# One-hot matrices of an expert-weight spread: token by token with contiguous columns, in place of four tokens interleaved

## The chip, the cores and the metric

The kernel runs on one core of one Trainium2 chip. A core has a matrix engine (TensorE; PE in the profile, with its weight loads listed apart as PEld), a vector engine (VectorE, DVE), a scalar engine (ScalarE, ACT), GpSimd (POOL) and a queue engine that issues most transfers (SyncE, SP). Each engine works through its own list of instructions in the order in which they stand and waits on semaphores. The metric is the device time of one execution in microseconds, lower being better; the time of a kernel is the median of three runs.

## The reference

Two transformer blocks run over 512 tokens of 1024 channels, in float32. The change lies in the last part of the second block, a product-key expert layer. For each token eight heads each choose 16 of 128 x 128 = 16384 experts, and each choice has a softmax weight:

```python
    s = jnp.einsum('thpd,pkd->thpk', q, sub_keys).astype(jnp.float32)
    s_top, i_top = lax.top_k(s, K)
    cand = (s_top[:, :, 0, :, None] + s_top[:, :, 1, None, :]).reshape(T, PEER_HEADS, K * K)
    cand_idx = (i_top[:, :, 0, :, None] * PEER_N_KEYS + i_top[:, :, 1, None, :]).reshape(T, PEER_HEADS, K * K)
    best, pos = lax.top_k(cand, K)
    eidx = jnp.take_along_axis(cand_idx, pos, axis=-1)
    g = jax.nn.softmax(best, axis=-1)
...
        u = expert_u[ib]
        a = jax.nn.gelu(jnp.einsum('thkd,td->thk', u, xb).astype(jnp.float32), approximate=False)
        w = (gb * a).astype(expert_v.dtype)
        return jnp.einsum('thk,thkd->td', w, expert_v[ib])
```

So a token has 128 triples (i, j, g): the two key numbers of an expert and its weight.

## The kernel before

Everything before the expert layer (two feed-forward blocks and two attention mixers) is left as it is. In the expert layer the first 128 tokens (tile 0) fetch their experts' rows one by one (`gather`, lines 1440 to 1458, issued by POOL, each row of products summed on DVE as `junk`). The other three tiles of 128 tokens are done densely: all 16384 experts are multiplied with the 384 tokens, in 128 chunks of 128 experts, and each result is multiplied with the token's weight for that expert, which is zero for most. One chunk is `emit_a`: 1024 weight columns are split into a high and a low part (`whi` on ACT at L120, `wlo` on DVE at L121), then 24 products of 384 columns run on PE (L126 to L128), then comes a gelu on ACT (`ga`).

For the dense part the weights g must lie in memory as a table [expert, token]. `peer_level2` (DVE alone) finds the 128 triples of each token of a tile, and `peer_spread` writes them out. For each token it makes two one-hot matrices with one row per triple: `oi` marks the triple's i, `oj` its j, and `og` is `oj` times g, in two float16 parts. Their product on PE, `oi` transposed times `og`, summed over the two parts, has each g at its place (i, j). DVE makes the matrices for eight tokens at a time by four instructions (`oi`, `oj`, `og` twice). Then PE runs 16 pairs of a weight load (`oi` of a token) and a matmul (`og` of that token, 128 columns) at L1383, ACT copies each four tokens out of PSUM into `gb` (L1386), and SP sends every 16 tokens to memory. That is 768 pairs of load and matmul over three tiles. `oi` and both `og` have two buffers each, `oj` one.

Work is written so that chunks of `emit_a` stand between: six before each tile's `peer_level2`, two after each 16 tokens. A scheduler then sets the order of every engine's list when the program is built; at run time the lists are fixed. The raw weights have two buffers of two chunks each, `whi` and `wlo` three each. After the spread comes the dense loop over 128 chunks, which reads the table back.

Before the change the matrices of four tokens are interleaved: element (token t, column j) of a group of four lies at 4 j + t, so that DVE reads the four tokens' values as a run, and PE reads a token's 128 columns in steps of four elements.

Of the kernel before, what the change touches and what calls it, by code (L numbers as in the profile page):

```python
# [9 lines left out]
F32 = mybir.dt.float32  # L10
F32R = mybir.dt.float32r
BF = mybir.dt.bfloat16
F16 = mybir.dt.float16
# [7 lines left out]
P = 128  # L21
# [60 lines left out]
class Body:  # L82
# [4 lines left out]
    # ---------------------------------------------------------------- helpers  # L87
# [3 lines left out]
    def banks(self, **tags):  # L91
        """Cut the eight PSUM banks into rings."""
        assert sum(tags.values()) == 8
        if self.bank_stack is not None:
            self.bank_stack.close()
        self.bank_stack = ExitStack()
        self.rings = {t: self.pool(self.bank_stack, "psum_" + t, bufs=n, space=PSUM, reuse_waits="tile")
                      for t, n in tags.items()}
# [42 lines left out]
    def rstd(self, ms, width=1, eps=EPS):  # L141
        """(ms + eps)^-1/2 of mean squares."""
# [8 lines left out]
    def sumsq(self, ap, n):  # L151
        """Sum over the row of its squares over n."""
# [5 lines left out]
    def xrstd(self, t):  # L158
        """1 / rms of the rows of x; the column that follows them brings EPS in."""
        return self.rstd(self.sumsq(self.xe[:, t, :D + 1], D), eps=0.0)  # L160

    def diag(self, r):
        """diag(r), as the right side of a transposing product."""
# [7 lines left out]
    # ---------------------------------------------------------------- set-up  # L171
# [88 lines left out]
    # ---------------------------------------------------------------- modulation  # L260
    def mod_unit(self, which, u, fast=False, tag="mod"):
        """256 columns of the modulation product, as columns over partitions."""
# [52 lines left out]
    def acol(self, i, sc, g, ks=slice(0, 8)):  # L315
        """(1 + sc) * g as columns."""
# [3 lines left out]
    def row_out(self, colv, tag="ps"):  # L320
        """A [128, 8] column vector, as a row in DRAM."""
# [9 lines left out]
    def row_in(self, d, tag="grow"):  # L331
        """The row over all partitions."""
# [12 lines left out]
    def begin(self, hi, lo):  # L345
        """Shift and scale of the first norm, h and the first products of the first swiglu,
        256 channels at a time."""
# [54 lines left out]
    # ---------------------------------------------------------------- norms  # L402
# [5 lines left out]
    def transposed(self, src, n, t, hi, lo, scale=None, bias=None, k0=0, tag="ps", diag=None):  # L408
        """src [128 t, n*128] -> hi/lo [128, k, 512 t] at tile t, each k scaled (and shifted) by a column,
        each row scaled by a diagonal matrix where one is given."""  # L410
# [29 lines left out]
    def boundary(self, join, scale, bias, last):  # L440
        """From one product to the next phase: last(t) emits the end of the product of a token tile, join(t)
        its way into x; then x is normed and turned, the second half of it later, by the steps returned."""
# [15 lines left out]
    def postnorm(self, t, y, grow):  # L458
        """x[t] += rms_norm(y) * grow, y two banks."""
# [11 lines left out]
    # ---------------------------------------------------------------- swiglu  # L471
    def ffn(self, gu, dn, h, between, join, scale, bias, ps0=None):
        """join(t, y) takes the two PSUM banks of a token tile; returns the next h and its pending steps."""
        nc = self.nc
        (hi, lo), late_h = h
        with ExitStack() as st:
            pool = self.pool(st, "ffn", reuse_waits="tile")
            # the modulation's weights pass through where the last four chunks will lie
# [64 lines left out]
    # ---------------------------------------------------------------- products  # L543
    def nform(self, ap, x, width, then, kd=KD, late=None):
        """[t, width] = x^T-tiles @ unit; then(t, psum) per token tile. The unit is [p, kd, width].
        The first of a phase goes token tile by token tile, as they come, with the steps that bring them."""
# [20 lines left out]
    def rope(self, src, out, half, j, heads):  # L567
        """src [128, heads, 2*half] (PSUM or SBUF) -> out, tables of tile j."""
# [14 lines left out]
    def attend(self, work, seg, scale, po, mneg, sums, n):  # L583
        """One softmax over one segment (lhsT, rhs, masks, values) as three stages to emit: the
        scores and their exponentials, their transposes, and the product with the values, left unnormalised in po."""
# [33 lines left out]
    def pipeline(self, chains, skews=(0, 3, 4)):  # L619
        """Emit the stages of the chains, each so many chains later; yields in between."""  # L620
# [6 lines left out]
    def merge(self, main, filler, n):  # L627
        """Emit n steps of the filler after each step of main, and what is left of it at the end."""
# [14 lines left out]
    # ---------------------------------------------------------------- first mixer  # L643
    def mixer1(self, u, late):
        """Returns the two branches' outputs [t, .] and the stack that holds them."""
# [47 lines left out]
    def latents(self, ap, cols, u, pa, at, late=None):  # L693
        """Columns of u @ w_in into pa[:, t, at:at+cols]."""
# [4 lines left out]
    def dsa_prep(self, pool, u, qT, kT, vv, qix, kix, wi, late):  # L699
# [4 lines left out]
        # columns: 256 of c_kv | 384 of c_q | k_rope, k_idx, w_idx, zeros  # L704
# [36 lines left out]
    def indexer(self, pool, qix, kix, wi, mk):  # L741
        """Additive masks of the selected keys, of the query blocks past the first."""
# [35 lines left out]
    def k_nope(self, w, kd, x, kT):  # L778
        """Rows 0..63 of every head, two heads at a time."""
# [8 lines left out]
    def q_rope(self, ap, kd, x, qT, qix, pos0):  # L788
        """Rotary parts of all heads (and of the indexer, where qix is given)."""
# [29 lines left out]
    def dilated(self, work, dil, u, ob, more):  # L819
        """Three dilated groups, two heads at a time; yields in between."""  # L820
# [72 lines left out]
    def dil_join(self, work, po, neg, sums, out):  # L893
        """The groups weighed by their shares of the joint softmax."""
# [51 lines left out]
    def gate(self, r, u, p):  # L946
        """One gate of 128 channels; yields in between."""
# [7 lines left out]
    def combine1(self, u, oa, ob, st):  # L955
        """z^T as a pair, then y banks."""
# [48 lines left out]
    def project(self, ap, z, pool, join, scale, bias):  # L1005
        """y = z^T tile @ four units of 256 columns, two banks a token tile; join, scale, bias as in ffn."""
# [26 lines left out]
    # ---------------------------------------------------------------- second mixer  # L1033
    def mixer2(self, h, st, late):
# [4 lines left out]
        # values and gates of the retention are made beside the attention  # L1039
# [665 lines left out]
```

## Time and profile before

| | us |
|---|---|
| median of three runs | 2908.83 |
| the three runs | 2907.96 to 2914.29 |
| span of the profiled execution, first to last instruction | 2905.4 |
| PE busy in it | 2848.4 (98%) |
| DVE busy in it | 2055.1 (71%) |
| ACT busy in it | 1156.0 (40%) |
| POOL busy in it | 368.6 (13%) |

The profile gives the execution's own time as its span alone; the median of the runs lies 3.4 us above it (start and end of the program). Busy time of an engine is the union of its instructions. [...]

### The profile page before, as it was taken

To read this page: it belongs to the slowest core of one execution; us is meant where nothing else is said; L and a number is where in the kernel's file an instruction comes from. 1 tells how busy PE (TensorE), PEld (TensorE's weight loads), DVE (VectorE), ACT (ScalarE), POOL (GpSimd) and SP (SyncE) were. 2 spreads that over 40 slices of the span, in tenths; PEclk is the share of its full clock that TensorE was granted. 3 is DMA by queue.
4 is the path that set the end of the run, shared out by engine and by line. 5 is a ranking of instruction groups with operands and counts; after the bars stand their busy time and mean duration, and the time that the engine had idled before them with its cause. 6 is when DMAs were issued, how large, how long until landed. Compare 5 with 4: busy or idle time off the path is not lost. (4 is left out here: it accounts for less than half of the span.)

```text
span 2905.4 us, 41181 instructions
## 1 busy us (share of the span) xinstructions
PE 2848.4 (98%) x15725; PEld 2454.6 (84%) x15725; DVE 2055.1 (71%) x4416; ACT 1156.0 (40%) x1946; POOL 368.6 (13%) x367
## 2 busy tenths in 40 slices
PE   8999999999999999999999999999999999999998
PEld 6877788878779877888899888999998888989986
DVE  6795246886566786236665799898867778878787
ACT  4343144333534443235422433655543333333333
POOL 0000000000000000001011002111111115444341
PEclk9999999999999999999998999999999999999999
DMA  6663222222042564221122227777889989888885
GB/s 274 226 228 137 92 73 80 73 68 89 16 148 110 207 229 168 99 87 62 55 74 75 93 100 262 267 250 264 283 312 350 324 316 342 337 297 322 310 322 192
DMA packets 152533, 553.09 MB, mean 190 GB/s; under 512 B 12368, under 2 KB 61840, under 8 KB 112400
## 3 DMA queue, kind: packets, MB, share of 16 engines
q1 hardware_dynamic: 111040, 404.25, 38.1%
q0 software_dynamic: 38848, 140.56, 13.6%
q10 hardware_dynamic: 2448, 5.65, 0.5%
q8 instruction: 123, 2.02, 0.3%
q14 instruction: 74, 0.61, 0.1%
HBM read 505.95 MB, written 44.47 MB: 189 GB/s over the span
## 5 line engine op out<-in xcount | busy, mean ns | idle before, releaser
L120 ACT ACTIVATE whi<-raw 128x1024 fp32r<-128x1024 f32 (+2 forms) x491 | 510.2, 1040 | 833.6 <-PE ps L127 405.2
L121 DVE TENSOR_TENSOR wlo<-raw,whi 128x1024 fp32r<-128x1024 f32 (+2 forms) x491 | 588.8, 1200 | 327.0 <-ACT whi L120 318.0
L126 PE MATMUL ps<-h_hi,whi 128*128 128x384 f32 (+2 forms) x1904 | 692.1, 364 | 4.1 <-ACT ga L1431 2.5
L128 PE MATMUL ps<-h_hi,wlo 128*128 128x384 f32 (+2 forms) x1904 | 683.1, 359 | 2.6 <-DVE wlo L121 2.6
L127 PE MATMUL ps<-h_lo,whi 128*128 128x384 f32 (+2 forms) x1904 | 684.3, 359 | 0.8 <-DVE h_lo L132 0.8
L126 PEld LDWEIGHTS ps<-h_hi,whi 128*128 128x128 f32 x1904 | 360.0, 189 | 37.4 <-ACT ga L1431 3.5
L128 PEld LDWEIGHTS ps<-h_hi,wlo 128*128 128x128 f32 x1904 | 359.4, 189 | 34.8 <-DVE wlo L121 3.3
L127 PEld LDWEIGHTS ps<-h_lo,whi 128*128 128x128 f32 x1904 | 360.0, 189 | 31.3 <-DVE h_lo L132 1.0
L128 PE MATMUL acc<-whi,wl 128*128 128x512 f32 x768 | 302.7, 394 | 0.0
L126 PE MATMUL acc<-whi,wh 128*128 128x512 f32 x768 | 302.6, 394 | 0.0
L127 PE MATMUL acc<-wlo,wh 128*128 128x512 f32 x768 | 302.5, 394 | 0.0
L1446 POOL DMA_INDIRECT erow<-in_eu,ids x128 | 142.1, 1110 | 686.0 <-DVE junk L1450 501.0
L131 ACT ACTIVATE wh<-wv 128x384 fp32r<-128x384 f32 x128 | 67.3, 526 | 337.0 <-issue 184.0
L1446 POOL DMA_INDIRECT erow<-in_ev,ids x128 | 167.0, 1305 | 225.1 <-DVE eacc L1458 199.9
L126 PE MATMUL ps<-whi,h_hi 128*128 128x256 f32 (+1 forms) x608 | 186.3, 307 | 0.0
L127 PE MATMUL ps<-wlo,h_hi 128*128 128x256 f32 (+1 forms) x608 | 184.4, 303 | 0.0
L128 PE MATMUL ps<-whi,h_lo 128*128 128x256 f32 (+1 forms) x608 | 184.0, 303 | 0.0
L128 PEld LDWEIGHTS acc<-whi,wl 128*128 128x128 f32 x768 | 143.7, 187 | 35.4
L127 PEld LDWEIGHTS acc<-wlo,wh 128*128 128x128 f32 x768 | 143.7, 187 | 33.4 <-DVE wlo L121 0.2
L126 PEld LDWEIGHTS acc<-whi,wh 128*128 128x128 f32 x768 | 143.6, 187 | 33.3 <-ACT whi L120 0.4
L1458 DVE SCALAR_TENSOR_TENSOR eacc<-erow,wgt,eacc 128x1024 f32<-128x1024 f32 x127 | 162.7, 1281 | 6.0 <-DMA erow<-in_ev,ids 4.4
L290 DVE SCALAR_TENSOR_TENSOR rows<-mraw,sil,rows 128x256 f32<-128x256 f32 x336 | 159.8, 481 | 6.5
(453 smaller groups left out, 4721.4 us busy)
## 6 DMA issues: line engine op xcount, KB each, us to landing
raw<-in_euT SPq DMA_DIRECT2D x64, 1024.0 KB
raw<-in_evp SPq DMA_DIRECT2D x64, 1024.0 KB
raw<-in_gu SPq DMA_DIRECT2D x44, 1024.0 KB
mraw<-in_wmod SPq DMA_DIRECT2D x24, 1024.0 KB
mraw<-in_wada SPq DMA_DIRECT2D x24, 1024.0 KB
dg<-gb SPq DMA_DIRECT2D x24, 1024.0 KB
gt<-dg SPq DMA_DIRECT2D x16, 1536.0 KB
raw<-in_dn SPq DMA_DIRECT2D x22, 1024.0 KB
```

The lines of the kernel that those rows point to most:

```text
L120: self.nc.scalar.activation(hi, r, AF.Copy)
L121: self.last_low = self.nc.vector.tensor_tensor(lo, r, hi.bitcast(F32), op=OP.subtract)
L126: mm(out, l[0], r[0], start=start, stop=False)
L127: mm(out, l[0], r[1], start=False, stop=False)
L128: self.last_mm = mm(out, l[1], r[0], start=False, stop=stop)
L131: self.nc.scalar.activation(hi, v, AF.Copy)
L290: nc.vector.scalar_tensor_tensor(rows, rv[:, k, :], c, rows, op0=OP.mult, op1=OP.add)
L1446: nc.gpsimd.indirect_dma_start(out=row, out_offset=None, in_=src, in_offset=bass.IndirectOffsetOnAxis(ap=ids[:, m:m + 1], axis=0))
L1458: nc.vector.scalar_tensor_tensor(eacc, row, wg[:, m:m + 1], eacc, op0=OP.mult, op1=OP.add)
```

## The change

The matrices of a token now lie in one piece: `oi`, `oj` and `og` are [token, 128 columns] for eight tokens, and PE reads 128 neighbouring columns. For DVE to still read runs of four, the values of a token (`it`, `jt`, `g1`, `g2`) are written four times next to each other when they come out of PSUM, so that these four small instructions are four times as wide (512 in place of 128 elements per partition), and the column numbers `io` are no longer repeated (128 in place of 512). The counts of all instructions stay. The diff's other lines remove comments.

```diff
-        g1 = sp.tile([P, P], F16, name="g1")
-        g2 = sp.tile([P, P], F16, name="g2")
-        nc.scalar.activation(g1, p[:, 256:384], AF.Copy, scale=16384.0)
-        nc.vector.scalar_tensor_tensor(g2, p[:, 256:384], 16384.0, g1, op0=OP.mult, op1=OP.subtract)
-        it, jt = sp.tile([P, P], F16, name="it"), sp.tile([P, P], F16, name="jt")
-        nc.scalar.activation(it, p[:, 0:P], AF.Copy)
-        nc.scalar.activation(jt, p[:, P:2 * P], AF.Copy)
-        ios = io[:, None].to_broadcast([P, 2, P, 4])
+
+        it, jt, g1, g2 = (sp.tile([P, P, 4], F16, name=n) for n in ("it", "jt", "g1", "g2"))
+        four = lambda k: p[:, k * P:(k + 1) * P, None].to_broadcast([P, P, 4])
+        nc.scalar.activation(g1, four(2), AF.Copy, scale=16384.0)
+        nc.vector.scalar_tensor_tensor(g2, four(2), 16384.0, g1, op0=OP.mult, op1=OP.subtract)
+        nc.scalar.activation(it, four(0), AF.Copy)
+        nc.scalar.activation(jt, four(1), AF.Copy)
+        ios = io.rearrange("p (o k f) -> p o k f", o=1, f=4).to_broadcast([P, 8, 32, 4])
...
-                row = [z[:, t0:t0 + 8].rearrange("p (h o t) -> p h o t", h=2, o=1).to_broadcast([P, 2, P, 4])
-                       for z in (it, jt, g1, g2)]
-                new = lambda n, m: sp.tile([P, 2, P, 4], F16, name=n, tag=n, bufs=m)
+                row = [z[:, t0:t0 + 8, None, :].to_broadcast([P, 8, 32, 4]) for z in (it, jt, g1, g2)]
+                new = lambda n, m: sp.tile([P, 8, P], F16, name=n, tag=n, bufs=m)
+                wide = lambda z: z.rearrange("p t (k f) -> p t k f", f=4)
                 oi, oj, og = new("oi", 2), new("oj", 1), [new("og0", 2), new("og1", 2)]
-                nc.vector.tensor_tensor(oi, ios, row[0], op=OP.is_equal)
-                nc.vector.tensor_tensor(oj, ios, row[1], op=OP.is_equal)
-                nc.vector.tensor_tensor(og[0], oj, row[2], op=OP.mult)
-                nc.vector.tensor_tensor(og[1], oj, row[3], op=OP.mult)
+                nc.vector.tensor_tensor(wide(oi), ios, row[0], op=OP.is_equal)
+                nc.vector.tensor_tensor(wide(oj), ios, row[1], op=OP.is_equal)
+                nc.vector.tensor_tensor(wide(og[0]), wide(oj), row[2], op=OP.mult)
+                nc.vector.tensor_tensor(wide(og[1]), wide(oj), row[3], op=OP.mult)
...
-                            nc.tensor.matmul(pg[:, t * P:(t + 1) * P], oi[:, h, :, t], og[k][:, h, :, t],
+                            nc.tensor.matmul(pg[:, t * P:(t + 1) * P], oi[:, 4 * h + t], og[k][:, 4 * h + t],
                                              start=k == 0, stop=k == 1)
...
-            io = sp.tile([P, P, 4], F16, name="io")
-            iof = self.misc.tile([P, P, 4], F32, name="iof", tag="xn", bufs=1)
-            nc.gpsimd.iota(iof, pattern=[[1, P], [0, 4]], base=0, channel_multiplier=0,
-                           allow_small_or_imprecise_dtypes=True)
+            io = sp.tile([P, P], F16, name="io")
+            iof = self.misc.tile([P, P], F32, name="iof", tag="xn", bufs=1)
+            nc.gpsimd.iota(iof, pattern=[[1, P]], base=0, channel_multiplier=0, allow_small_or_imprecise_dtypes=True)
             nc.scalar.activation(io, iof, AF.Copy)
```

The scheduler places some instructions anew. On PE, at the beginning of tile 1's spread, the difference of the lists reads as follows (`sc` are PSUM banks, `oi` and `og` the matrices of the first eight tokens, the other rows are products of an `emit_a` chunk):

```order
@@ -8974,4 +8974,7 @@
 L128 MATMUL ps<-h_hi,wlo 128x384
 L126 MATMUL ps<-h_hi,whi 128x384
+L127 MATMUL ps<-h_lo,whi 128x384
+L128 MATMUL ps<-h_hi,wlo 128x384
+L126 MATMUL ps<-h_hi,whi 128x384
 L1383 LDWEIGHTS oi
 L1383 MATMUL sc<-og_16676,oi 128x128
@@ -8980,5 +8983,4 @@
 L127 MATMUL ps<-h_lo,whi 128x384
 L128 MATMUL ps<-h_hi,wlo 128x384
-L126 MATMUL ps<-h_hi,whi 128x384
 L1383 LDWEIGHTS oi
 L1383 MATMUL sc<-og_16677,oi 128x128
```

The first pair of the spread stands three products later and the next pairs two products earlier; the rest of the tile goes on in the same alternation, two pairs, two or three products, 14 pairs, nine to twelve products.

On DVE, the list of the changed kernel at the same place (`g` is the second part of the weights, `wlo` the split of a chunk, `junk` the gather's sum, `cand` belongs to the next tile's `peer_level2`):

```order
L121 TENSOR_TENSOR wlo<-raw,whi 128x1024
L1363 SCALAR_TENSOR_TENSOR g_16668<-sc,g_16667 128x512
L1450 SCALAR_TENSOR_TENSOR junk,act<-erow,xr 128x1024
L1375 TENSOR_TENSOR oi<-io,it 128x1024
L1376 TENSOR_TENSOR oj<-io,jt 128x1024
L1375 TENSOR_TENSOR oi<-io,it 128x1024
L1377 TENSOR_TENSOR og_16676<-oj,g_16667 128x1024
L1378 TENSOR_TENSOR og_16677<-oj,g_16668 128x1024
L121 TENSOR_TENSOR wlo<-raw,whi 128x1024
L1376 TENSOR_TENSOR oj<-io,jt 128x1024
L1375 TENSOR_TENSOR oi<-io,it 128x1024
L1377 TENSOR_TENSOR og_16704<-oj,g_16667 128x1024
```

Nothing moved here: only the width of `g` (and its line) differs from the kernel before. The `oi` of a group stands ahead of the `og` of the group before it.

## Rows read from the trace of the kernel before

**Rows 1.** The page: the span.

```profile
span 2905.4 us, 41181 instructions
```

**Rows 2.** Stretches of the spread: length, busy us (instructions) by engine, clock, DMA.

```profile
core 0: us, PE busy (x) PEld busy (x) DVE busy (x) ACT busy (x) POOL busy (x), PEclk, DMA share, GB/s
1813.00:1876.00 63.00, 63.00 (x433) 58.30 (x432) 52.60 (x79) 39.29 (x46) 5.72 (x5) 1.00 0.70 258
1876.00:1921.00 45.00, 44.09 (x264) 42.92 (x262) 43.13 (x157) 21.86 (x30) 7.72 (x7) 1.00 0.74 265
1921.00:2013.00 92.00, 91.67 (x608) 88.86 (x609) 81.71 (x192) 53.56 (x64) 11.74 (x11) 1.00 0.72 254
2013.00:2046.00 33.00, 33.00 (x197) 32.57 (x197) 23.49 (x43) 12.30 (x20) 5.13 (x6) 1.00 0.83 306
2046.00:2131.00 85.00, 85.00 (x567) 82.36 (x565) 61.52 (x90) 48.79 (x58) 9.89 (x9) 1.00 0.75 267
```

**Rows 3.** Three of these stretches, matmuls and weight loads of L1383 alone.

```profile
1813.00:1876.00 63.00, 31.11 (x224) 23.24 (x224) 1.00 0.70 258
...
1921.00:2013.00 92.00, 32.97 (x256) 28.08 (x256) 1.00 0.72 254
...
2046.00:2131.00 85.00, 31.11 (x244) 26.50 (x241) 1.00 0.75 267
```

**Rows 4.** PE in order of time: start, us, instruction, how many in a row.

```profile
1814.24 1.81 PE L1383 MATMUL sc<-og,oi 128*128 128x128 f16 x14
...
1816.24 0.34 PE L126 MATMUL ps<-h_hi,whi 128*128 128x384 f32 x1
1816.42 0.34 PE L127 MATMUL ps<-h_lo,whi 128*128 128x384 f32 x1
```

**Rows 5.** Line L1383: count, ns least/median/most, first and last start.

```profile
L1383 PEld LDWEIGHTS <-oi x768: 112/117/138, 1813.5 to 2126.8; 128*128 128x128 f16 x192
L1383 PE MATMUL sc<-og,oi x768: 284/297/303, 1813.5 to 2126.9; 128*128 128x128 f16 x192
```

**Rows 6.** Line L595, a bfloat16 mask product in an earlier stage, likewise.

```profile
L595 PEld LDWEIGHTS <-idb x172: 95/98/257, 554.9 to 1440.7; 128*128 128x128 bf16 x172
L595 PE MATMUL ps<-masks,idb x148: 219/221/314, 554.9 to 1441.2; 128*128 128x128 bf16 x148
```

**Rows 7.** PE in order of time where four of these stand together.

```profile
620.49 0.40 PE L595 MATMUL ps<-masks,idb 128*128 128x128 bf16 x4
```

**Rows 8.** DVE in order of time, one group of eight tokens; [idle before, releaser].

```profile
1859.23 0.69 DVE L1375 TENSOR_TENSOR oi<-io,it 128x1024 f16<-128x1024 f16 x1 [0.73 <-PE sc L1383]
1859.84 0.68 DVE L1377 TENSOR_TENSOR og<-oj,g 128x1024 f16<-128x1024 f16 x1
...
1861.04 1.22 DVE L121 TENSOR_TENSOR wlo<-raw,whi 128x1024 fp32r<-128x1024 f32 x1
1862.18 0.68 DVE L1376 TENSOR_TENSOR oj<-io,jt 128x1024 f16<-128x1024 f16 x1
1863.76 0.69 DVE L1375 TENSOR_TENSOR oi<-io,it 128x1024 f16<-128x1024 f16 x1 [0.90 <-PE sc L1383]
```

**Rows 9.** Waits of DVE from 1800 to 2140: us in total, times, longest.

```profile
DVE wlo L121 <- ACT whi L120: 34.2, 23, 6.7
DVE oi L1375 <- PE sc L1383: 16.2, 21, 2.6
```

**Rows 10.** Lines of small instructions: count, ns least/median/most, first and last start.

```profile
L1362 DVE SCALAR_TENSOR_TENSOR g<-sc,g x3: 276/281/283, 1809.6 to 2039.9; 128x128 f16<-128x128 f32 x3
...
L1364 ACT ACTIVATE it<-sc x3: 277/277/277, 1809.9 to 2040.2; 128x128 f16<-128x128 f32 x3
...
L1479 ACT ACTIVATE io<-iof x1: 631/631/631, 1622.8 to 1622.8; 128x512 f16<-128x512 f32 x1
```

**Rows 11.** A stretch of the dense loop, columns as in rows 2.

```profile
2300.00:2700.00 400.00, 400.00 (x1914) 347.67 (x1913) 321.38 (x388) 139.88 (x192) 149.74 (x119) 1.00 0.88 321
```

## The prediction

> **What bounds the kernel now.** I read the page for the span, then the busy times by stretch to see which engine is full while the spread runs, then the rows of the changed lines, and last the waits between PE and DVE. The span is 2905.4 us [rows 1]; the median of the runs, 2908.8, lies 3.4 us above it. The spread runs from about 1813 to 2131. Of these 318 us PE is busy in 317, at full clock in every stretch, and DVE in 262 [rows 2]; the dense loop behind it keeps PE busy too, 400 of 400 us [rows 11]. So PE sets the end here and after, and a microsecond that leaves PE in the spread reaches the end, as long as no other engine takes its place. That "busy" is not hollow is seen from start to start: products of 384 columns follow each other in 0.17 to 0.18 us (1816.24, 1816.42) [rows 4], and only listed ends overlap. The nearest other engine is DVE. It is full where it finds the next tile's experts (43.1 of 45 us before 1921) and has most room in the last tile (61.5 of 85) [rows 2].
>
> **What the change does to PE.** 768 pairs of load and matmul read their columns in steps of eight bytes before, and neighbouring ones after. 14 of them in a row last 1.81 us [rows 4]; less the last one's own 0.297 [rows 5] that is 1.51 for 13, so 0.116 us from one to the next. For the same 128 columns of a two-byte type that lie together the trace has one kind of row, the mask product of L595: four last 0.40 us [rows 7], less 0.221 [rows 6] is 0.18 for three, so 0.060. The two also differ alone: a matmul of L1383 lasts 297 ns and one of L595 221, and the weight loads 117 and 98 [rows 5, 6]. The 76 ns stand in the matmul itself, which points at the columns that it streams and not at the load ahead of it. I take 0.060 for the pair after the change, as the nearest row in size, type width and form (a load for each matmul). Bounds: at 384 columns in 0.174 us a column costs 0.45 ns, so 128 can hardly go below 0.058; and if the layout isn't the cause at all, the pair stays at 0.116. PE so sheds 768 x 0.056 = 43 us, between 0 and 45.
>
> [...]
>
> [...]
>
> **What takes over.** DVE's instructions keep number, type, width and runs of four, so I leave oi, oj and og at their start-to-start 0.60 us (1859.23 to 1859.84) [rows 8]. In one group of eight tokens it does four of these and one instruction of 1.22 (a chunk's split, or a gather's sum), and then waits for PE to give a buffer of oi back: 1859.23 to 1863.76 is 4.53 us, of which 0.90 is that wait [rows 8]. Hence DVE alone needs 3.6 us a group, while PE, whose 16 pairs take 1.86 now, would come down by 0.9 to the same 3.6. Where groups follow each other like this, DVE is the next bound, and the gain is no more than its idle time. So I take stretch by stretch the smaller of two numbers: what PE sheds (count of pairs [rows 3] times 0.056) and what DVE idles (length less busy [rows 2]).
>
> 1813 to 1876: 224 pairs, 12.5; DVE idle 10.4; so 10.4. 1876 to 1921: the few pairs here shed 1.8, DVE idles 1.9; so 1.8. 1921 to 2013: 256 pairs, 14.3; DVE idle 10.3; so 10.3. 2013 to 2046: hardly any pairs (with the stretch before 1921 they are 768 - 224 - 256 - 244 = 44), 0.9. 2046 to 2131: 244 pairs, 13.7; DVE idle 23.5; so 13.7. Together 37.1 us.
>
> **What is added.** Three ACT copies per tile and one DVE instruction become four times as wide. On ACT 128 columns take 277 ns and 512 take 631 [rows 10], so 0.35 more each, 3.2 us over nine; ACT is busy 39 of 63 us in the fullest stretch [rows 2], and its own work hides it. The DVE one took 0.28 [rows 10]; it lies between that and the 0.69 of an oi, so up to 0.4 more, three times. They stand one behind another at a tile's head (weights, their second part, i, then oi), 0.35 + 0.4 + 0.35 = 1.1 us per tile if nothing covers them. A gather's sum stands between on DVE, and PE has three more products before the first pair. Between 0 and 3.3 us over three tiles I take 2, since at two heads DVE is itself full. If that cover went, it would be the 3.3. The column numbers `io` are made once at 1622, far before their use, and the 631 ns copy becomes shorter: no effect.
>
> The scheduler's shifts are of two or three products (0.17 us each) around a pair, in the same alternation; PE does the same work, so I cost them at nothing. Would PE wait at such a place, the price is 0.5 us a time.
>
> Two engines that are both nearly full hold each other up. Before, DVE's wait for oi came to 16.2 us in 21 waits, and its wait for ACT's high parts, which in turn wait for PE, to 34.2 [rows 9]; the former should go, the latter in part. I take off 3 us, some one per cent of the stretch, for idle time that stays on DVE where I counted none. That is a choice; the bound on it is that half of the 37 stays, 18.5.
>
> Sum: 37.1 - 2 - 3 = 32 us. 2905.4 - 32 = 2873 us of span, and with the 3.4 us around it 2877 us.
>
> Transfers: the stretch moves 254 to 306 GB/s [rows 2]. In 286 us in place of 318 the same bytes need a ninth more, 282 to 340; the dense loop carries 321 at a share of 0.88 [rows 11] with PE full. Raw weights are fetched two chunks ahead, so I count no wait.
>
> **Rivals.**
> 1. PE sheds all of it. DVE's room in the last tile and the fixed lists might let DVE run ahead further than stretch by stretch. Then 43 us go, 2866; with 45 and no added cost 2864. Against it: before 1921 DVE is at 43.1 of 45 us, and PE behind it would have to wait for the next tile's triples.
> 2. Reading isn't the cause. Steps of eight bytes would stream as fast as neighbouring columns, and the 0.116 would come from something that both layouts share, such as float16 or two products on the same columns of PSUM. For it: L595 is bfloat16 and there is no contiguous float16 row. Against: the products of L126 to L128 also fall three times on the same columns and hold 0.174 for 384. Then only the added 0 to 3 us are left: 2909 to 2912, 2910. [...]
> 3. VectorE falls back (slower). The new patterns repeat 128 column numbers eight times and four values 32 times; if the engine then took one element where it took two, an instruction of 1024 elements would cost like the split, 1.14 us from start to start (1861.04 to 1862.18) and not 0.60 [rows 8]. That is 192 x 0.54 = 104 us; DVE's 262 would become 366 against the 318 of now, 48 us slower, 2957. It decides once an instruction costs over (318 - 262) / 192 = 0.29 us more. Against it: runs of four two-byte elements are read before and after, and before they cost 0.60.
> 4. PE gains, but DVE and ACT are coupled worse than I count, by order or by waits at the tiles' heads: less than half of the 37, about 12 us, 2897.
>
> **How the numbers follow.** The forecast (20 to 38 us off, 2871 to 2889) has 0.62; rival 1 0.13; rival 2 0.12; rival 3 0.05; rival 4 0.08. About 0.2%, 5.8 us, is what a measurement of this kernel tells from no change. Faster: 0.62 + 0.13 + 0.08 = 0.83; same: 0.12; slower: 0.05. The range reaches down to rival 1 with its bound, 2864, less the 0.9 us by which the fastest run lies below the median, so 2863, and up to 2893, the bound of 18.5 us off with the added 3.3; rivals 2 and 3 and most of 4 are left out.
>
> **What would show it.** Right: 14 pairs of L1383 in a row at about 1.0 us in place of 1.81, a matmul near 221 ns; the waits of DVE for L1383 nearly gone; PE with some 10 us of idle time between 1813 and the end of the spread, mostly at a wait for DVE before the second tile; oi, oj and og at 0.60; the dense loop of the same length, begun about 32 us earlier. Wrong: pairs still at 0.116 (rival 2), instructions of 1.14 us on DVE (rival 3), PE without idle time (rival 1), or the time lost again in the dense loop, by transfers or gathers that came late there.

## The result and the profile after

The changed kernel takes 2867.02 us (median of four runs, 2863.69 to 2869.12) against 2908.39 us for the kernel before in the same rounds (four runs, 2905.51 to 2914.29). The ratio is 0.986 with a 95% interval from 0.9846 to 0.9875, so the change takes off 41.4 us. The forecast was a gain of 32 us, to 2877. The measured 2867 lies in the stated range (2863 to 2893) but outside the forecast's own 20 to 38 us; it has the size of rival 1, to which the prediction gave 0.13.

The page of the changed kernel begins with the span; the second line gives busy time, share and instructions of each engine.

```profile
span 2864.1 us, 41177 instructions
...
PE 2805.2 (98%) x15725; PEld 2414.2 (84%) x15725; DVE 2052.6 (72%) x4416; ACT 1158.3 (40%) x1946; POOL 366.7 (13%) x367
```

The span fell by 2905.4 - 2864.1 = 41.3 us, and PE's busy time by 43.2, from 2848.4. PE's and DVE's counts of instructions are the same, and the other engines' busy times changed by two or three microseconds: PE got less to do, and hardly anything was taken from or given to the others.

Line L1383 in the changed kernel, and 14 pairs in a row, the answers to [rows 5] and [rows 4]:

```profile
L1383 PEld LDWEIGHTS <-oi x768: 95/98/103, 1811.8 to 2081.2; 128*128 128x128 f16 x192
L1383 PE MATMUL sc<-og,oi x768: 216/219/231, 1811.8 to 2081.3; 128*128 128x128 f16 x192
```

```profile
1843.25 0.95 PE L1383 MATMUL sc<-og,oi 128*128 128x128 f16 x14
```

A pair now costs (0.95 - 0.219) / 13 = 0.056 us in place of 0.116. The matmul lost 78 ns (297 to 219), the load 19 (117 to 98).

The stretches of [rows 2] in the changed kernel, columns as there; PEclk is the clock granted to TensorE, as a share of the full one. The clock times are the same but the work in them is not: the third tile's spread, which began at 2040 before, now begins at 2009 and ends at 2081.

```profile
1813.00:1876.00 63.00, 63.00 (x517) 58.28 (x515) 63.00 (x142) 46.28 (x54) 7.85 (x7) 1.00 0.87 311
1876.00:1921.00 45.00, 43.21 (x293) 41.38 (x292) 44.76 (x111) 25.75 (x33) 7.20 (x7) 1.00 0.76 259
1921.00:2013.00 92.00, 92.00 (x658) 90.78 (x656) 86.34 (x211) 55.36 (x70) 15.79 (x14) 1.00 0.89 312
2013.00:2046.00 33.00, 33.00 (x272) 30.89 (x271) 32.97 (x50) 23.80 (x29) 3.44 (x3) 1.00 0.84 306
2046.00:2131.00 85.00, 83.03 (x518) 76.51 (x516) 61.93 (x91) 41.01 (x54) 16.78 (x15) 0.98 0.92 326
```

PE is still full, with 1.8 us of idle time before 1921 and 2.0 after 2046. DVE is now full beside it: 63.00 of 63 in the first stretch, where it had 52.6 before. Up to 2013 DVE idles 5.9 us in 200; it was 22.6.

One group of eight tokens on DVE, in order of time (answers to [rows 8]):

```profile
1851.94 0.67 DVE L1375 TENSOR_TENSOR oi<-io,it 128x1024 f16<-128x1024 f16 x1
1852.54 0.67 DVE L1377 TENSOR_TENSOR og<-oj,g 128x1024 f16<-128x1024 f16 x1
...
1853.74 1.21 DVE L121 TENSOR_TENSOR wlo<-raw,whi 128x1024 fp32r<-128x1024 f32 x1
1854.88 0.67 DVE L1376 TENSOR_TENSOR oj<-io,jt 128x1024 f16<-128x1024 f16 x1
1855.48 0.67 DVE L1375 TENSOR_TENSOR oi<-io,it 128x1024 f16<-128x1024 f16 x1
```

From one `oi` to the next it is 3.54 us in place of 4.53, with no wait in brackets, and the instructions keep their 0.60 from start to start. The waits of DVE from 1800 to 2140 (answers to [rows 9]) say the same: the wait of `oi` for L1383, 16.2 us, is gone from the list, and that for ACT's high parts is halved. The second row below stands in this stretch because the spread ends earlier; before the change DVE waited for that table at 2143, and for 1.1 us.

```profile
DVE wlo L121 <- ACT whi L120: 17.8, 10, 4.8
DVE wv L1543 <- DMA gt<-dg: 9.1, 2, 6.6
```

The widened copies at the head of each tile (answers to [rows 10]):

```profile
L1363 DVE SCALAR_TENSOR_TENSOR g<-sc,g x3: 674/683/683, 1807.4 to 2009.2; 128x512 f16<-128x512 f32 x3
L1364 ACT ACTIVATE it<-sc x3: 597/597/597, 1808.1 to 2010.0; 128x512 f16<-128x512 f32 x3
```

**Where the 41.3 us come from.** L1363 runs once at each tile's head, so its first and last start mark the start of tile 1 and of tile 3, in [rows 10] and above; the last pair of L1383 marks the end of the spread [rows 5]. Four pieces follow:

| piece | before | after | gained, us |
|---|---|---|---|
| up to tile 1's head | 1809.6 | 1807.4 | 2.2 |
| tiles 1 and 2 | 2039.9 - 1809.6 = 230.3 | 2009.2 - 1807.4 = 201.8 | 28.5 |
| tile 3 to the last pair | 2126.9 - 2039.9 = 87.0 | 2081.3 - 2009.2 = 72.1 | 14.9 |
| from the last pair to the end | 2905.4 - 2126.9 = 778.5 | 2864.1 - 2081.3 = 782.8 | -4.3 |

The first piece is mostly scatter: the instruction that makes the column numbers (L1477, ahead of every changed pair) starts at 1621.6 in the profile before, at 1619.7 here, and between 1615.2 and 1622.0 in the ten further profiles. The three tiles give 43.4. PE's steps from start to start tell where these lie: from the first pair to the last, 705 steps from one pair to the next took 82.8 us before and 40.0 after, 63 steps from the last pair of a row to a product 2.9 and 1.8, and everything else 227.8 and 227.7. So PE shed 43.9 us there and lost nothing elsewhere in the spread. And 4.3 are given back behind the last pair. That piece is no scatter: it takes 782.4 to 783.9 us in the profiles of e1, e3, e5, e6 and e8, whose pairs are fast, and 778.6 and 779.8 in those of e2 and e7, whose pairs are as before.

**The piece given back.** Behind the spread comes the dense loop, whose first step needs the table that the spread has just written. The instructions of SP's queue around that point, before the change and then after it (`dg` is the table in memory, `gt` the part read back for eight chunks, `gb` 16 tokens of it):

```profile
2128.39 0.32 SPq L1388 DMA_DIRECT2D dg<-gb  x1
...
2133.79 0.38 SPq L1542 DMA_DIRECT2D gt<-dg  x1
```

```profile
2084.68 0.32 SPq L1388 DMA_DIRECT2D dg<-gb  x1
2091.39 0.38 SPq L1541 DMA_DIRECT2D gt<-dg  x1
```

Before, the last piece of the table was sent 1.5 us after the last pair (2126.9) and the read went out 5.4 us later. After, it was sent 3.4 us after the last pair (2081.3), since ACT's copies out of PSUM now come behind the faster pairs:

```profile
2080.90 3.75 ACT L1386 ACTIVATE gb<-sc 128x512 f32<-128x512 f32 x4
```

The read then went out 6.7 us later. DVE's `wv` waits 6.6 us for it, ACT's `wh` (its rounding) for `wv`, and PE, whose chunks made ahead have run out, for `wh`. PE in order of time at the first products of the dense loop (`acc`), and the windows there (columns as in [rows 2]):

```profile
2102.04 0.34 PE L128 MATMUL ps<-h_hi,wlo 128*128 128x384 f32 x1
...
2104.03 0.50 PE L126 MATMUL acc<-whi,wh 128*128 128x512 f32 x1 [1.66 <-ACT wh L131]
...
2105.52 0.63 PE L126 MATMUL acc<-whi,wh 128*128 128x512 f32 x1
2105.95 0.63 PE L127 MATMUL acc<-wlo,wh 128*128 128x512 f32 x1
```

```profile
2100.00:2104.00 4.00, 2.37 (x14) 2.05 (x12) 1.14 (x2) 0.55 (x2) 0.00 (x0) 1.00 1.02 417
2104.00:2108.00 4.00, 3.65 (x9) 2.61 (x10) 4.00 (x8) 1.83 (x3) 2.10 (x2) 0.66 0.68 225
2108.00:2112.00 4.00, 4.00 (x17) 3.19 (x16) 4.00 (x8) 3.21 (x5) 1.61 (x2) 0.91 1.01 395
```

PE waits 1.66 us, and behind the wait the granted clock falls to 0.66, a mean over part of the window at 0.50 (all of 2106 to 2107) and part at 1.00: the products at 2105.52 and 2105.95 stand 0.43 us apart, and from 2109.76 on, at 1.00, such products follow each other in 0.23 to 0.24. The shortfall of clock is 4 x 0.34 + 4 x 0.09 = 1.7 us, so by this estimate wait and clock cost about 3.4 of the 4.3 in this profile (e5 below gives back nearly as much without the lower clock). In the kernel before PE passed this place without a gap:

```profile
2147.68 0.34 PE L128 MATMUL ps<-h_hi,wlo 128*128 128x384 f32 x1
2147.86 0.39 PE L126 MATMUL acc<-whi,wh 128*128 128x512 f32 x1
```

### The profile page after: what moved, and what is told of

Read it like the earlier page. It is cut to its first block, busy times and chain, and to the rows that moved or that the text cites. A ratio compares the mean times of both kernels' runs of the same rounds, so it can differ in the third digit from the quotient of the medians.

```text
span 2864.1 us, 41177 instructions
## 1 busy us (share of the span) xinstructions
PE 2805.2 (98%) x15725; PEld 2414.2 (84%) x15725; DVE 2052.6 (72%) x4416; ACT 1158.3 (40%) x1946; POOL 366.7 (13%) x367
## 3 DMA queue, kind: packets, MB, share of 16 engines
q8 instruction: 123, 2.02, 0.3%
```

## The experiments

Ten further runs were made, one of them the changed kernel once more; all compute the whole result. Those with a ratio are set against runs of the kernel before on the same chip.

**1. Which read pays.** Theory A: the matmul pays for the columns of `og` that it streams. Theory B: the weight load pays for the columns of `oi`. So one of the two is laid out contiguously and the other left interleaved by four. Experiment e1 makes `oj` and `og` contiguous:

```diff
-                oi, oj, og = new("oi", 2), new("oj", 1), [new("og0", 2), new("og1", 2)]
-                nc.vector.tensor_tensor(wide(oi), ios, row[0], op=OP.is_equal)
...
+                vi, vg = four8, flat8
+                nc.vector.tensor_tensor(vi(oi), four4, ri, op=OP.is_equal)
+                nc.vector.tensor_tensor(vg(oj), flat, row[0], op=OP.is_equal)
...
-                            nc.tensor.matmul(pg[:, t * P:(t + 1) * P], oi[:, 4 * h + t], og[k][:, 4 * h + t],
+                            nc.tensor.matmul(pg[:, t * P:(t + 1) * P], one(oi, 4 * h + t, False), one(og[k], 4 * h + t, True),
```

> Only the streamed matrices (oj, og) lie token by token; the loaded one (oi) stays interleaved by four. Theory A (the matmul's own read of its streamed columns was slow): pairs of L1383 at 0.056 to 0.060 us from start to start, matmul near 219 ns, about 2867 us like the changed kernel. Theory B (the weight load's stepped read held the pairs): pairs stay at 0.116, about 2908 us. Theory C (each of the two reads holds the pairs by itself): pairs between, still 0.1 or more.

Experiment e2 makes `oi` alone contiguous (`vi, vg = flat8, four8`, and the flags of `one` the other way round).

> Only the loaded matrix (oi) lies token by token; the streamed ones (oj, og) stay interleaved by four. Theory A (streamed read): pairs stay at 0.116 us, matmul 297 ns, load 98 ns in place of 117, about 2908 us. Theory B (load): pairs at 0.056 to 0.060, about 2867 us.

Measured: e1 2863.4 us (2862.95 to 2867.18, four runs), ratio 0.9855, interval 0.9839 to 0.9872; e2 2904.42 us (2900.53 to 2906.95, ten runs), ratio 0.9989, interval 0.998 to 0.9999. Line L1390 is the pair in both. First e1, with 32 pairs in a row:

```profile
L1390 PEld LDWEIGHTS <-oi x768: 111/113/138, 1809.3 to 2079.3; 128*128 128x128 f16 x192
L1390 PE MATMUL sc<-og,oi x768: 218/219/252, 1809.3 to 2079.4; 128*128 128x128 f16 x192
```

```profile
2046.96 1.98 PE L1390 MATMUL sc<-og,oi 128*128 128x128 f16 x32
```

Then e2:

```profile
L1390 PEld LDWEIGHTS <-oi x768: 95/115/118, 1813.8 to 2124.5; 128*128 128x128 f16 x192
L1390 PE MATMUL sc<-og,oi x768: 273/294/296, 1813.8 to 2124.6; 128*128 128x128 f16 x192
```

In e1 a pair costs (1.98 - 0.219) / 31 = 0.057 us although the load is still listed with 113 ns; so the listed loads overlap what stands next to them, and their time does not add to the pair's. In e2 the matmul keeps its 294 ns, and 14 pairs last 1.79 us, 0.115 each. Theory A holds, theories B and C fall. One expectation was missed: the load of e2, now of neighbouring columns, was to take 98 ns and is listed with 115, as long as the interleaved load of e1. So these listed times of a load, 113 ns for interleaved columns and 115 for neighbouring ones beside a matmul of 294, do not tell how the load's own columns lie. Half of the change, the layout of `oj` and `og`, gives all of the gain that can be measured.

**2. How the price depends on the step.** Counted in lines of 16 bytes, the layout before has two columns of a token in each line of memory. Two tokens interleaved instead of four (e3) put four columns there, eight tokens (e4) one. Whether such a line means anything to TensorE is what the runs are to show.

```diff
-        ios = io[:, None].to_broadcast([P, 2, P, 4])
+        ios = io[:, None].to_broadcast([P, 4, P, 2])
...
-                new = lambda n, m: sp.tile([P, 2, P, 4], F16, name=n, tag=n, bufs=m)
+                new = lambda n, m: sp.tile([P, 4, P, 2], F16, name=n, tag=n, bufs=m)
```

This is e3 against the kernel before; e4 has `[P, 1, P, 8]` in the same places.

> The kernel before with two tokens interleaved in place of four, in all four matrices: PE reads columns four bytes apart. If any step over neighbouring elements halves the rate: pairs 0.116 us and 2908 us. If the cost follows how few of the columns share a 16-byte line (four of them here, two at a step of eight bytes, eight when contiguous): pairs 0.056 to 0.08, 2867 to 2885 us. [...]

> The kernel before with eight tokens interleaved: PE reads columns 16 bytes apart, one in each 16-byte line. If any step halves the rate: pairs 0.116 us, about 2908 us. If the cost follows the number of lines: pairs about 0.23 us, PE needs 768 x 0.115 = 88 us more, about 2990 us.

Measured: e3 2867.46 us (2863.08 to 2869.6, four runs), ratio 0.9862, interval 0.9846 to 0.9879; e4 3030.43 us (3025.91 to 3031.67, four runs), ratio 1.0421, interval 1.0404 to 1.0439. PE in order of time, 32 pairs in a row, in e3 and then in e4:

```profile
2039.81 2.02 PE L1383 MATMUL sc<-og,oi 128*128 128x128 f16 x32
```

```profile
2042.52 7.69 PE L1383 MATMUL sc<-og,oi 128*128 128x128 f16 x32
```

With matmuls of 219 ns a pair of e3 costs (2.02 - 0.219) / 31 = 0.058, as good as contiguous. With matmuls of 413 ns a pair of e4 costs (7.69 - 0.413) / 31 = 0.235, twice the price before. DVE's instructions of 1024 elements took 0.69 us in both, with runs of two as with runs of eight values.

The time of e4 is 40 us above what had been expected. It lost 123 us against the kernel before, of which 768 x (0.235 - 0.116) = 91 would be the pairs by their price. The windows of e4 show the rest (columns as in [rows 2]):

```profile
1813.00:1960.00 147.00, 146.17 (x683) 122.14 (x681) 93.31 (x232) 63.42 (x74) 13.40 (x12) 0.88 0.51 184
1960.00:2125.00 165.00, 164.62 (x787) 141.18 (x786) 103.51 (x231) 69.29 (x82) 16.80 (x16) 0.87 0.57 199
2125.00:2250.00 125.00, 125.00 (x567) 101.53 (x566) 65.29 (x93) 53.45 (x59) 9.85 (x9) 0.83 0.52 185
```

PE is listed as busy throughout, with waits of 1.2 us in all, and yet its clock is granted at 0.83 to 0.88 for as long as the slow pairs run, and at 1.00 from 2270 to 2400. These are means of two levels, 0.50 and 1.00: the shortfall in the three windows, 147 x 0.12 + 165 x 0.13 + 125 x 0.17, is 60 us, so of the 437 us from the first pair to the last 120 were granted at 0.50. The products between the pairs suffer there. PE in order of time behind the row of 32 pairs above, first at 0.50 (2047 to 2053), then at 1.00 (2054 to 2063):

```profile
2050.64 0.52 PE L128 MATMUL ps<-h_hi,wlo 128*128 128x384 f32 x1
2050.96 0.52 PE L126 MATMUL ps<-h_hi,whi 128*128 128x384 f32 x1
...
2053.81 0.33 PE L127 MATMUL ps<-h_lo,whi 128*128 128x384 f32 x1
2053.98 0.33 PE L128 MATMUL ps<-h_hi,wlo 128*128 128x384 f32 x1
```

A product costs 0.32 us at the low level and 0.17 at the high one. The pairs take the same at both, 0.234 and 0.235 in the median. Over the spread the steps from product to product took 254.2 us in e4 and 214.2 in the kernel before, 40.0 more; those from pair to pair 166.1 and 82.8, 83.3 more. Together they are the 123 us. So the missing time is that of products at the lower clock. Why the clock falls among the slow pairs no run isolates; that stays open.

**3. Lines touched, or bytes passed.** Steps of 4, 8 and 16 bytes differ both in the lines of 16 bytes that hold the 128 columns and in the bytes that they span. A step of 32 bytes tells these apart: as many lines as at 16 bytes (128), twice the bytes. Theory F: the price goes by lines, so 0.235 again. Theory G: by bytes, so it doubles. Against e4:

```diff
-                oi, oj, og = new("oi", 2), new("oj", 1), [new("og0", 2), new("og1", 2)]
+                half = lambda n: sp.tile([P, 1, P, 16], F16, name=n, tag=n, bufs=1)[:, :, :, 0:8]
+                oi, oj, og = new("oi", 2), new("oj", 1), [half("og0"), half("og1")]
```

> As the run with eight tokens interleaved, but the columns of og lie 32 bytes apart (eight of sixteen slots used), and each og has one buffer, so that only the pair's time is to be compared. Theory F (the streamed read pays for each 16-byte line that it touches; at 16 bytes it touches one per column already): pairs stay at 0.234 us. Theory G (it pays for the bytes it passes over): pairs at 0.45 to 0.47 us.

Measured: 3017.49 us in a single run, beside 2905.91 for the kernel before; only the pair's time is read from it. The line of the pair, and 16 pairs in a row:

```profile
L1384 PE MATMUL sc<-og,oi x768: 411/415/452, 1807.0 to 2237.7; 128*128 128x128 f16 x192
```

```profile
2049.78 3.97 PE L1384 MATMUL sc<-og,oi 128*128 128x128 f16 x16
```

(3.97 - 0.415) / 15 = 0.237, as theory F expected; theory G falls. The pairs of all runs side by side:

| step of the streamed columns, bytes | columns in a line of 16 bytes | lines touched | us a pair |
|---|---|---|---|
| 2 (changed kernel, e1) | 8 | 16 | 0.056, 0.057 |
| 4 (e3) | 4 | 32 | 0.058 |
| 8 (before, e2) | 2 | 64 | 0.116, 0.115 |
| 16 (e4) | 1 | 128 | 0.235 |
| 32 (e10) | 1 | 128 | 0.237 |

0.116 / 64 and 0.235 / 128 are both 1.8 ns a line; the floor of 0.056 us is 0.44 ns a column, close to the 0.45 that the prediction read from products of 384 columns. By 1.8 ns a line 32 lines would come to 0.058, about that floor. The length of 16 bytes is read from these five steps: the price doubles from 8 bytes to 16 and stays from 16 to 32. No step in between was run.

**4. Is VectorE the bound now?** The same needless work on DVE, half of `oj` written a second time in every group, is put into both kernels. 48 times half of an `oj`'s 0.68 us are 16 us.

```diff
                 nc.vector.tensor_tensor(wide(oj), ios, row[1], op=OP.is_equal)
+                nc.vector.tensor_tensor(wide(oj)[:, 0:4], ios[:, 0:4], row[1][:, 0:4], op=OP.is_equal)
```

That is e8, against the changed kernel; e7 adds the like to the kernel before, and e5 is the changed kernel once more, in the same rounds.

> The changed kernel as it is, beside the next run. In its trace PE reaches the end of the spread 45.6 us earlier than before and the dense loop only 41.6 us earlier, with a wait for the first weight table (gt) in between. Theory D (the table is read back too late, since the chunks that cover it did not grow): the same wait of 2 us on PE and the lower clock behind it are here again, time 2863 to 2869 us. Rival: the wait is an accident of one execution and is not here.

> The kernel before, in which DVE writes one half of oj a second time in each group of eight tokens (48 instructions of 512 elements, 0.34 us each from start to start, 16 us in all). Theory E (DVE has room before the change, some 0.7 us a group): 0 to 3 us slower.

> The changed kernel with the same 48 extra DVE instructions. Theory E (after the change DVE sets the pace in tiles 1 and 2, and has room only in tile 3): the extra work of 32 groups comes through, 8 to 11 us slower than the changed kernel, seen as waits of PE for og; in tile 3 nothing. Rival (PE still sets the pace everywhere, and DVE only looks full because it fills its time): 0 to 3 us slower, as for the kernel before.

Measured against 2906.84 us for the kernel before: e5 2865.41 (2864.15 to 2867.3, four runs), ratio 0.9863, interval 0.9846 to 0.9879; e7 2908.48 (2905.97 to 2912.3, ten runs), ratio 1.0011, interval 1.0001 to 1.002; e8 2874.62 (2869.18 to 2875.13, four runs), ratio 0.9887, interval 0.9868 to 0.9905. So the same 16 us cost 1.6 us before, which is within 0.2%, and 9.2 after. Two windows of e8, then one of e7:

```profile
1813.00:1876.00 63.00, 63.00 (x501) 57.98 (x499) 63.00 (x115) 43.34 (x52) 8.02 (x7) 1.00 0.82 296
...
1921.00:2013.00 92.00, 92.00 (x678) 86.55 (x677) 91.75 (x228) 59.74 (x72) 13.34 (x12) 1.00 0.84 296
```

```profile
1813.00:1876.00 63.00, 63.00 (x423) 58.96 (x422) 54.86 (x97) 37.74 (x44) 8.02 (x7) 1.00 0.71 251
```

In e8 DVE is full where it was full and also from 1921 to 2013, where it had 5.7 us left; in e7 it still has 8.1 of 63 free. The waits of PE for `og` that had been expected of e8 came at the weight loads of the pairs, from 1800 to 2140; in the changed kernel the like came to 4.3 us in 24 waits.

```profile
PEld L1384 <- DVE og L1378: 9.3, 45, 0.3
```

Part of the 9.2 is scatter from ahead of the spread, where the instruction that makes the column numbers starts at 1621.5 in e8 and at 1618.0 in e5. Of the 10.5 us by which the two profiles' spans differ 7.0 lie behind it; for e7 and the kernel before (1619.4 and 1621.6) it is 2.4. So the same work costs more after the change: DVE's room is mostly used up. It is not shown that DVE alone sets the pace, since PE's steps in the changed kernel have no gaps to speak of either. Nor is the place shown. Between the tiles' first transposes tile 1 of e8 grew by 2.5 us, tile 2 not at all and tile 3, up to the last pair, by 4.7; between the heads at L1363, as in the table above, tiles 1 and 2 grew by 5.6 together and tile 3 by 1.1.

**5. The 4.3 us at the head of the dense loop.** If PE waits there because it has too little work of its own left, two chunks more made ahead should fill the gap (e6). If the chain behind the table's read ends last in any case, the wait moves. e5 shows first that the wait is no accident: PE waits there again, 1.8 us for `wh`, before its product at 2103.1. But the lower clock that had been expected with the wait is missing: 1.00 is granted from 2098 to 2114. The piece from the last pair to the end takes 782.4 us all the same, as in e1, whose clock does not fall there either. So the loss does not need the lower clock. In e5 PE idles 3.1 us from the last pair to the last product of the dense loop, and not at all in the kernel before.

```diff
-        LEAD, EARLY = 12, 78
+        LEAD, EARLY = 12, 80
```

> The changed kernel with 80 chunks of emit_a ahead of the dense loop in place of 78, so that two more (8.3 us of PE) stand between the last pairs and the first product that needs the table. Theory D: PE does not wait there, its clock stays at 1.00, and 3 to 4 us go, 0.12 to 0.14% below the changed kernel of this call. Rival (the loss is not that wait but transfers that are short of bandwidth there): the wait moves to the next table or to the weights, and the time is within 1 us of the changed kernel.

Measured: 2863.8 us (2863.51 to 2867.71, four runs), ratio 0.9859, interval 0.9842 to 0.9877, not to be told from e5. From the last pair to the end it is 783.1 us in e6 and 782.4 in e5. PE in order of time:

```profile
2101.91 0.48 PE L126 MATMUL ps<-h_hi,whi 128*128 128x384 f32 x1 [1.94 <-ACT ga L1431]
```

Neither expectation came as written. PE still waits, but no longer for the table: it now stands before a chunk's product, which needs a PSUM bank back from the gelu `ga`, and in ACT's list the `wh` that waits for the table stands ahead of that gelu. The extra chunks don't help while ACT itself is held.

So e9 makes the read of the table earlier. The first one is cut in three, one for each tile, so that two thirds of it need not wait for the last piece written.

```diff
-                nc.sync.dma_start(gt, dg[:, :, c:c + 8, :].rearrange("g i j t -> i g j t"))
+                for z in ([slice(8 * k, 8 * k + 8) for k in range(3)] if c == 0 else [slice(0, NG)]):
+                    nc.sync.dma_start(gt[:, z], dg[z, :, c:c + 8, :].rearrange("g i j t -> i g j t"))
```

> The changed kernel, in which the first load of the weight table (gt) is cut into three, one per token tile, so that two of them need not wait until the last write of the table has landed. Theory D2 (the wait at the head of the dense loop is the chain of last write, 6 us, and first load, 11 us): gt is whole before PE has done its 121 products, the wait of 2 us on PE and the lower clock behind it are gone, 2.5 to 4 us less than the changed kernel, about 2862. Rival (bandwidth is short there, three loads take as long as one): gt lands at the same time, no difference.

Measured: 2863.9 us (2857.52 to 2866.95, five runs), ratio 0.9851, interval 0.9835 to 0.9866. The profiled execution has a span of 2858.8 us. SP's queue, and the window in which PE had waited:

```profile
2082.05 0.32 SPq L1388 DMA_DIRECT2D dg<-gb  x1
2082.46 7.63 SPq L1542 DMA_DIRECT2D gt<-dg  x3
```

```profile
2100.00:2104.00 4.00, 4.00 (x19) 3.21 (x18) 4.00 (x8) 2.03 (x4) 1.95 (x2) 1.00 0.98 341
```

The table's first use (`wv`) now comes 17.3 us behind the last pair (2096.0 less 2078.7), in place of 21.6 in the changed kernel and 16.1 in the kernel before. PE no longer waits, and its clock stays at 1.00 in every window of four microseconds from 2092 to 2116. From the last pair to the end it is 780.1 us, 2.7 less than in the changed kernel and below all five profiles named above, 1.6 more than before. In the medians of the runs the 2.7 can't be seen: 2863.9 against 2867.02 and 2865.41, with intervals that overlap. e9 beats the kernel before for certain, the changed kernel not for certain.

## Why the prediction came out as it did

**PE's pair.** Right in cause and nearly in size: 0.060 was taken from L595 [rows 7], 0.056 was measured, a little below the bound of 0.058. A pair so sheds 0.060 and not 0.056, but the 63 pairs in front of a product shed only 0.018 each. These two errors cancel, and that the 43 us came so near the 43.9 measured is in part luck. The reading of the streamed matrix was named as the cause, and e1 (0.057 us a pair) and e2 (0.115) show it. At steps of eight bytes a pair costs 0.116 us, at steps of four 0.058 (e3). Rival 2 falls with it: the 0.116 did not come from float16 or from PSUM, which all the kernels share.

**VectorE's own price.** Right: `oi`, `oj` and `og` stayed at 0.60 us from start to start, so rival 3 falls, and a group came to 3.54 us where 3.6 was counted. DVE did become full, as said.

**The minimum stretch by stretch.** This is the step that failed, and it was a term's size. The prediction took 37.1 us, the sum over five stretches of the smaller of PE's shed and DVE's idle time. In tiles 1 and 2 that gave 10.4 + 1.8 + 10.3 = 22.5 (the 0.9 from 2013 to 2046 belongs to tile 3, whose first pair stands at 2043.8); measured were 28.5. PE shed 28.9 of its 43.9 there, and DVE's idle time over the four stretches together was 32.1 [rows 2]. So the minimum over both tiles, 28.9, is what came, within 0.4. The 9.5 us that DVE idled from 2013 to 2046 had been left out because hardly any pairs stand there. What that idle time was, the waits of DVE and then of ACT in this stretch of the kernel before tell:

```profile
DVE wlo L121 <- ACT whi L120: 9.4, 6, 2.9
```

```profile
ACT whi L120 <- PE ps L127: 15.1, 6, 2.7
```

DVE waited for ACT's high parts and ACT for PE to give their buffers back. Read so, it was a wait for PE at one remove, which goes when PE has less to do: from 1800 to 2140 DVE's wait for the high parts fell from 34.2 us [rows 9] to 17.8. This is read from the waits; no run changed that chain alone. Tile 3 gave 14.9 where 0.9 + 13.7 = 14.6 was counted.

**The deductions.** 2 us were taken off for the wider copies at the tiles' heads. They took their time (683 ns where 281 stood, 597 where 277 did), and from the first transposes to the first pair the three heads grew by 1.65 us together, about half of it PE's longer wait in tile 2 named below; but PE had products to do there, and its steps outside the pairs took no longer in all. So the 2 us did not come. 3 us were taken off for idle time that stays on DVE. 5.9 us did stay, from 1813 to 2013, but DVE had had 32.1 from 1813 to 2046 and not the 22.5 counted, and PE's waits grew by 0.9 us alone.

**PE's idle time.** Some 10 us were expected in the spread, mostly before tile 2. PE idled 1.8 there (0.9 before the change), at the wait named: its first transposes of tile 2 waited for DVE's numbers `gi` from L1336. For the rest it stayed full, which was rival 1's sign. Rival 1 gave the right size, 43 off, and its reason, DVE ahead of PE across stretches, is the one that the waits point to. Its counter-argument, that PE would have to wait for the next tile's triples, was true for 1.8 us alone.

**The dense loop.** Costed at nothing. It gave 4.3 us back, at a place that the prediction named only in its last sentence. So 43.4 - 4.3 = 39.1, and with the 2.2 that lie ahead of the change 41.3. e9 shows that 2.7 of the 4.3 go when the table's read is no longer late; that rests on one profile. What the other 1.6 are stays open, and they are less than the scatter of the runs.

## What to carry to other kernels

Two engines that wait for each other can share their idle time over the whole loop that couples them, and here did, not slice by slice: before taking the minimum of what one sheds and the other has free, look whether the second one's idle time is itself a wait for the first, since that part may come free with it. When a matrix is laid out to please the engine that writes it, price the engine that reads it too, from the start-to-start time of its rows; here interleaving by two would have served both (0.058 us a pair and 0.69 us a DVE instruction in e3), by four it cost TensorE double (0.116 us a pair). And a stage that ends earlier can hand its last result to the next one with less cover, as here (4.3 us given back), so follow the chain behind its last instruction, copies and transfers included.

## What the runs showed of the hardware

The price of the matmul's streamed read followed the lines of 16 bytes that held its 128 columns: a pair took 0.116, 0.235 and 0.237 us for 64, 128 and 128 lines (the kernel before, e4, e10), 1.8 ns a line in each, and 0.056 and 0.058 for 16 and 32 lines (the changed kernel, e3), 0.44 to 0.45 ns a column. The weight load of interleaved columns cost nothing that could be measured: in e1 it is listed with 113 ns, and the pair takes 0.057 us. Its listed time grew to 146 ns in e4, but not by its own step alone, as the 115 ns of neighbouring columns in e2 show.

TensorE's clock was granted at 0.83 to 0.88 over 437 us in e4 while the engine was listed as busy in 436 of them, so a full busy row did not go with a full clock. In the 120 us at 0.50 a product of 384 columns took 0.32 us from start to start in place of 0.17, while the pairs took 0.234 and 0.235 in the median at the two levels.
